# Seven block products in place of eight for the first matrix product of an MLP, inside a whole transformer layer

## The chip, the cores and the metric

The kernel runs on one core of one Trainium2 chip. The metric is the device time of one execution in microseconds (us), as the median of several runs. The core's engines are TensorE (PE), VectorE (DVE), ScalarE (ACT), GpSimd (POOL) and SyncE (SP, which here issues the DMA transfers). Each engine works off its own queue in order.

## What is computed

One layer over 2048 tokens of width 1024: a token mixer (RWKV and differential attention), then a gated MLP with a convolution over neighbouring tokens. The change touches the MLP alone:

```python
def conv_ffn(h, p):
    u = dwconv(h @ p['w_up'], p['ffn_conv']) + p['ffn_conv_b']     # w_up 1024 x 5632, three taps over tokens
    val, gate = jnp.split(u, 2, axis=-1)                           # 2816 columns each
    return (val * jax.nn.silu(gate)) @ p['w_down']                 # w_down 2816 x 1024

h = modulate(rmsnorm(x, p['g_pre_ffn']), sh2, sc2)
x = x + gt2 * rmsnorm(conv_ffn(h, p), p['g_post_ffn'])
```

All of it is in 32-bit floats.

## The kernel before

A matrix product of 32-bit numbers is made of three matmuls: each operand is split into a rounded part H and a rest L (`split`: ScalarE casts to H, then VectorE or GpSimd subtracts to get L), and `split_mm` adds H·H, H·L and L·H in PSUM. The kernel is written in a framework that puts in the waits between engines and chooses the order of the instructions in each engine's queue; the program gives an order of preference.

The function `phase45` is the MLP. Tokens go in 16 tiles of 128, or in 4 blocks of 512. Columns of w_up go in tiles of 128: column tile j (22 of them) has a half for `val` and one for `gate`.

First product. `ttiles` loads a tile of the residual stream x1, norms it (`row_stats`), transposes it on TensorE, scales it and splits it into the transposed activations, which all stay in SBUF (`h2H`, `h2L`, for the 4 blocks). The first four tiles are made while the phase before (`phase23`, the output projection of the mixer) is ending; the other twelve are made beside the matmuls of column tile 0. For each j and each half, `wload` loads 1024 x 128 weights (512 KB) and splits them, the subtraction on GpSimd; `mblock` runs 8 x 3 matmuls of 512 columns for each block and ScalarE copies the result to the tile `cs` (one row of 2048 tokens and a border on each side). `finish` makes the convolution and the gate from `cs` on VectorE (with one activation on ScalarE) in two pieces of 1024 tokens, and stores the result to DRAM (`actT`).

Second product. The 2816 rows of w_down are taken in two groups of 11 tiles. `dload` loads a row tile of w_down (512 KB) and splits it into the buffers that held h2H and h2L; `aload` loads and splits the activations of a token tile. For each group and token tile 11 x 2 x 3 matmuls run. The first group's results are copied to SBUF (`parts`); the second group's are added to them, normed and added to x1.

Of the kernel before, what the change touches and what calls it, by code (L numbers as in the profile page):

```python
# [8 lines left out]
F32 = mybir.dt.float32  # L9
# [1545 lines left out]
NH = NF // 2  # L1555
NT = SEQ // P
BORD = [0, 1, 2, 3]


def phase45(tc, I, T, pr, keep, ident, out):  # L1560
# [3 lines left out]
    st, sx = ExitStack(), ExitStack()  # L1564
    wp = st.enter_context(tc.tile_pool(name="wu", bufs=2, side="right"))
    hb = {BORD[0]: st.enter_context(tc.tile_pool(name="h2a", bufs=1, side="right"))}
    pss = [st.enter_context(tc.tile_pool(name="ps4a", bufs=1, space=PSUM, side="right"))]
    xp = sx.enter_context(tc.tile_pool(name="x4", bufs=1, side="right"))
    pt = sx.enter_context(tc.tile_pool(name="pst4", bufs=3, space=PSUM, side="right"))
    hH, hL = {}, {}  # L1570
# [3 lines left out]
    def pst():  # L1574
        pss.append(pss.pop(0))
        return pss[-1].tile([P, BLK], F32, name="o4")

    def new_h(b):
        hH[b], hL[b] = [hb[b].tile([P, KT, BLK], F32R, name="h2%s%d" % (s, b)) for s in "HL"]

    def wring():
        return (wp.tile([P, KT, P], F32, name="wuraw"), wp.tile([P, KT, P], F32R, name="wuH"), wp.tile([P, KT, P], F32R, name="wuL"))
# [5 lines left out]
    def wload(c0):  # L1588
        raw, H, L = wring()
        nc.sync.dma_start(out=raw, in_=wv[:, :, c0:c0 + P])  # L1590
        split(raw, H, L, nc.gpsimd)
        return H, L

    def stile(n):
        S = sp.tile([P, SEQ + 2], F32, name="cs%d" % n)
        nc.gpsimd.memset(S[:, 0:1], 0.0)
        nc.gpsimd.memset(S[:, SEQ + 1:SEQ + 2], 0.0)
        return S

    def mblock(W, S, b):  # L1600
        o = pst()
        for k in range(KT):
            split_mm(nc, o, W[0][:, k], W[1][:, k], hH[b][:, k], hL[b][:, k], k == 0, k == KT - 1)
            if k % 2 and k < KT - 1:
                yield
        nc.scalar.copy(out=S[:, 1 + b * BLK:1 + (b + 1) * BLK], in_=o)  # L1606
        yield

    def finish(j, Ss):
        for b in range(2):  # L1610
            t0 = b * 1024
            Os = []
            for n in (1, 0):
                w = [col[("fconvg%d" if n else "fconv%d") % t][:, j:j + 1] for t in range(3)]
                O = cv.tile([P, D], F32, name="co%d" % n)
                S = Ss[n]
                nc.vector.tensor_scalar(out=O, in0=S[:, t0:t0 + 1024], scalar1=w[0], scalar2=None, op0=ALU.mult)  # L1617
                nc.vector.scalar_tensor_tensor(out=O, in0=S[:, t0 + 1:t0 + 1025], scalar=w[1], in1=O, op0=ALU.mult, op1=ALU.add)
                nc.vector.scalar_tensor_tensor(out=O, in0=S[:, t0 + 2:t0 + 1026], scalar=w[2], in1=O, op0=ALU.mult, op1=ALU.add)
                if n:  # L1620
                    nc.scalar.activation(out=O, in_=O, func=AF.Silu, bias=col["fbias1"][:, j:j + 1])
                Os.append(O)
            nc.vector.scalar_tensor_tensor(out=Os[1], in0=Os[1], scalar=col["fbias0"][:, j:j + 1], in1=Os[0], op0=ALU.add, op1=ALU.mult)
            nc.sync.dma_start(out=T["actT"][j * P:(j + 1) * P, t0:t0 + 1024], in_=Os[1])

    tiles = [4 * b + t for b in BORD for t in range(4)]
    xq = {}

    def xload(m):
        if m < NT:  # L1630
            xq[m] = xp.tile([P, D], F32, name="xs4", bufs=4)
            nc.sync.dma_start(out=xq[m], in_=T["x1"][tiles[m] * P:(tiles[m] + 1) * P])

    def ttiles(m0, m1):
        for m in range(m0, m1):
            b, t = divmod(tiles[m], 4)
            z = (keep["gs2"], keep["sh2"], hH[b], hL[b], t * P, ident)
            transpose_half(nc, xp, pt, "tpx4", xq[m], 0, *z)
            if m + 2 < NT:
                row_stats(nc, xp, xp, xq[m + 2], mh)  # L1640
            yield
            transpose_half(nc, xp, pt, "tpx4", xq[m], 4, *z, nc.gpsimd)
            xload(m + 4)
            yield

    new_h(BORD[0])
    for m in range(4):
        xload(m)
    Ws = [wload(0), wload(DFF)]
    for m in range(2):  # L1650
        row_stats(nc, xp, xp, xq[m], mh)
    yield
    yield from ttiles(0, 4)
    yield "early"

    sp = st.enter_context(tc.tile_pool(name="cs4", bufs=1))
    hp = st.enter_context(tc.tile_pool(name="h2b", bufs=1))
    pss.extend([st.enter_context(tc.tile_pool(name="ps4b", bufs=4, space=PSUM))] * 4)
    for b in BORD[1:]:
        hb[b] = hp  # L1660
        new_h(b)
    Ss = [stile(0), stile(1)]

    def both(b):
        for n in range(2):
            yield from mblock(Ws[n], Ss[n], b)

    for m, b in enumerate(BORD):
        gens = [both(b)]
        if m < 3:  # L1670
            gens.append(ttiles(4 * m + 4, 4 * m + 8))
        robin(gens)
    sx.close()
    cv = st.enter_context(tc.tile_pool(name="cv", bufs=2))
    fp = st.enter_context(tc.tile_pool(name="fp5", bufs=1))
    pss.extend([st.enter_context(tc.tile_pool(name="ps4c", bufs=3, space=PSUM, side="right"))] * 3)
    finish(0, Ss)
    for j in range(1, NF):
        if j < NF - 1:
            Ss = []  # L1680
            for n in range(2):
                W = wload(n * DFF + j * P)
                S = stile(n)
                for b in range(4):
                    robin([mblock(W, S, b)])
                Ss.append(S)
        else:
            Ws = [wload(j * P), wload(DFF + j * P)]
            Ss = [stile(0), stile(1)]
            for n, b in ((0, 0), (0, 1), (1, 0), (1, 1), (0, 2), (0, 3), (1, 2), (1, 3)):  # L1690
                robin([mblock(Ws[n], Ss[n], b)])
        finish(j, Ss)

    acts, Wg = {}, {}

    def aload(a, t):
        r8, H8, L8 = wring()
        r3, H3, L3 = [fp.tile([P, NH - KT, P], d, name="a3" + s, bufs=2) for s, d in (("r", F32), ("H", F32R), ("L", F32R))]
        ts = slice(t * P, (t + 1) * P)
        nc.sync.dma_start(out=r8, in_=av[:, a * NH:a * NH + KT, ts])  # L1700
        nc.sync.dma_start(out=r3, in_=av[:, a * NH + KT:(a + 1) * NH, ts])
        split(r8, H8, L8, nc.gpsimd)
        split(r3, H3, L3, nc.gpsimd)
        acts[a, t] = [(H8[:, k], L8[:, k]) for k in range(KT)] + [(H3[:, k], L3[:, k]) for k in range(NH - KT)]

# [21 lines left out]
    for k in range(2, NH):  # L1727
        dload(0, k)
# [12 lines left out]
    for i, (a, t) in enumerate(steps):  # L1741
        if (a, t) == (0, NT - 3):
            draw(1, 0)
# [136 lines left out]
```

## Time and profile before

| | |
|---|---|
| time, median of 3 runs | 4140.62 us (4139.7 to 4144.2) |
| the profiled execution: span from first to last instruction | 4140.8 us |
| PE busy | 3824.6 us (92%), 25471 matmuls |
| DVE busy | 2671.8 us (65%) |
| ACT busy | 1881.5 us (45%) |
| POOL busy | 1543.3 us (37%) |
| moved by DMA | 400.80 MB, mean 97 GB/s |
| mean granted TensorE clock | 0.960 of full speed |

The profiled execution has nothing beside its span, which is as long as the median of the runs. A busy time is the sum of the durations of an engine's instructions, and a duration holds the time in which an instruction that has started stands still. Matmuls are pipelined: the records of neighbours overlap, so a matmul's cost is the distance to the next one, not its duration. "L1617" is a line of the kernel. `o<-h2H,wuH` names the tile that is written and those that are read.

### The profile page before, as it was taken

The page shows a single profiled execution, that of the slowest core. Times are in us where ns is not written, and L with a number is a line of the kernel's source. Part 1 is how long each engine was busy: PE and PEld are TensorE (multiplying, and loading weights), DVE is VectorE, ACT ScalarE, POOL GpSimd, SP SyncE. Part 2 cuts the span into 40 slices and gives each one's busy share as a digit, 9 for nine tenths or more (in the row PEclk, how much of TensorE's full clock was granted, in tenths as well). Part 3 has the DMA queues.
Part 4 walks back from the last instruction along what each step waited for, and adds up shares of the span by engine and source line. Part 5 has one row for each costly group of instructions (what it writes and reads, how often), then busy time and mean ns, then how long its engine had stood idle before and what let it go on. Part 6 is the DMA issues. An engine that isn't in the chain of part 4 may idle for free. (4 is left out here: it accounts for less than half of the span.)

```text
span 4140.8 us, 65493 instructions
## 1 busy us (share of the span) xinstructions
PE 3824.6 (92%) x25471; PEld 3213.6 (78%) x25471; DVE 2671.8 (65%) x3869; ACT 1881.5 (45%) x3678; POOL 1543.3 (37%) x1617
## 2 busy tenths in 40 slices
PE   7998888897899987989999899899999999999999
PEld 4777666676888876888898778788888888878887
DVE  3467678978889886888989868754444444420243
ACT  4235454466666656777777644521112112221211
POOL 3237467844444433455444366511101101022222
PEclk8999999998999988999999999999999999999999
DMA  4554546554434333020102163311111111131333
GB/s 174 160 168 154 162 146 214 205 161 94 97 95 101 94 85 101 8 61 22 33 6 74 51 219 136 117 61 51 46 43 62 46 41 56 51 101 44 115 114 102
DMA packets 464724, 400.80 MB, mean 97 GB/s; under 512 B 131613, under 2 KB 393702, under 8 KB 463390
## 3 DMA queue, kind: packets, MB, share of 16 engines
q1 hardware_dynamic: 464414, 396.61, 31.3%
q8 instruction: 201, 3.29, 0.3%
q14 instruction: 109, 0.89, 0.1%
HBM read 269.51 MB, written 131.74 MB: 97 GB/s over the span
## 5 line engine op out<-in xcount | busy, mean ns | idle before, releaser
L36 PE MATMUL o<-h2H,wuL 128*128 128x512 f32 x1920 | 761.7, 397 | 0.8 <-POOL wuL L1586 0.8
L34 PE MATMUL o<-h2H,wuH 128*128 128x512 f32 x1920 | 755.5, 394 | 5.6 <-DVE h2H L179 3.7
L35 PE MATMUL o<-h2L,wuH 128*128 128x512 f32 x1920 | 759.1, 395 | 0.2 <-DVE h2L L180 0.2
L1586 POOL TENSOR_TENSOR wuL<-wuraw,wuH 128x1024 fp32r<-128x1024 f32 x76 | 182.2, 2399 | 871.0 <-ACT wuH L1585 871.0
L34 PEld LDWEIGHTS o<-h2H,wuH 128*128 128x128 f32 x1920 | 362.0, 189 | 90.8 <-DVE h2H L179 3.9
L35 PEld LDWEIGHTS o<-h2L,wuH 128*128 128x128 f32 x1920 | 361.9, 189 | 89.9 <-DVE h2L L180 1.6
L36 PEld LDWEIGHTS o<-h2H,wuL 128*128 128x128 f32 x1920 | 362.1, 189 | 83.5 <-POOL wuL L1586 1.5
L34 PE MATMUL mm<-hH,wH 128*128 128x512 f32 (+1 forms) x968 | 384.5, 398 | 23.1 <-DVE hH L179 13.0
L787 DVE TENSOR_REDUCE nb<-S 128x1 f32<-128x768 f32 x384 | 357.8, 948 | 54.1 <-PE S L786 52.8
L35 PE MATMUL mm<-hL,wH 128*128 128x512 f32 (+1 forms) x968 | 382.0, 395 | 1.0 <-DVE rstd L162 0.9
L788 ACT ACTIVATE P<-S,nb 128x768 f32<-128x768 f32 x384 | 345.8, 907 | 77.4 <-DVE nb L787 74.5
L36 PE MATMUL mm<-hH,wL 128*128 128x512 f32 (+1 forms) x968 | 380.9, 394 | 0.0
L1617 DVE TENSOR_SCALAR co<-cs,cols 128x1024 f32<-128x1024 f32 x88 | 139.8, 1590 | 314.4 <-ACT cs L1606 313.0
L785 PE MATMUL S<-kH,qs 128*128 128x384 f32 x768 | 293.4, 382 | 36.1 <-ACT P L788 33.8
L829 PE MATMUL pv<-V,aT 128*128 128x128 f32 x2304 | 310.0, 279 | 5.5 <-DVE O L845 3.0
L1606 ACT COPY cs<-o 128x512 f32<-128x512 f32 x176 | 103.0, 586 | 449.8 <-PE o L36 449.6
L829 PEld LDWEIGHTS pv<-V,aT 128*128 128x128 f32 x2304 | 286.6, 195 | 9.1 <-DVE O L845 5.8
L786 PE MATMUL S<-kL,qs 128*128 128x384 f32 x768 | 261.2, 340 | 0.0
L815 DVE SCALAR_TENSOR_TENSOR P<-P,f,P 128x768 f32<-128x768 f32 x192 | 243.9, 1283 | 12.5 <-POOL P L813 10.9
L34 PEld LDWEIGHTS mm<-hH,wH 128*128 128x128 f32 x968 | 191.1, 198 | 63.8 <-DVE hH L179 13.9
L35 PEld LDWEIGHTS mm<-hL,wH 128*128 128x128 f32 x968 | 191.5, 198 | 40.2 <-DVE hL L180 2.2
L36 PEld LDWEIGHTS mm<-hH,wL 128*128 128x128 f32 x968 | 191.4, 198 | 38.9 <-issue 0.7
(362 smaller groups left out, 8103.6 us busy)
## 6 DMA issues: line engine op xcount, KB each, us to landing
wraw<-in_w_in_dram SPq DMA_DIRECT2D x52, 512.0 KB
wuraw<-in_w_up_dram SPq DMA_DIRECT2D x44, 512.0 KB
scr_actT<-co SPq DMA_DIRECT2D x44, 512.0 KB
QP<-scr_qd SPq DMA_DIRECT2D x36, 512.0 KB
PK<-scr_pd SPq DMA_DIRECT2D x144, 128.0 KB
mww<-in_w_mod_dram SPq DMA_DIRECT2D x64, 256.0 KB
scr_pd<-G SPq DMA_DIRECT2D x32, 512.0 KB
scr_qd<-Q SPq DMA_DIRECT2D x32, 512.0 KB
```

The source lines that it names most:

```text
L34: nc.tensor.matmul(out, lhsT=lH, rhs=rH, start=first, stop=False)
L35: nc.tensor.matmul(out, lhsT=lH, rhs=rL, start=False, stop=False)
L36: nc.tensor.matmul(out, lhsT=lL, rhs=rH, start=False, stop=last)
L785: nc.tensor.matmul(S[:, b, 0:HB], lhsT=qs[:, qt * P:(qt + 1) * P], rhs=kH[:, sl], start=True, stop=False)
L786: nc.tensor.matmul(S[:, b, 0:HB], lhsT=qs[:, qt * P:(qt + 1) * P], rhs=kL[:, sl], start=False, stop=True)
L787: nc.vector.tensor_reduce(out=nb[:, m, g:g + 1], in_=S[:, :, 0:HB], op=ALU.max, axis=AX.XY, negate=True)
L788: nc.scalar.activation(out=Pm[m][:, g * GW:(g + 1) * GW].rearrange("p (b x) -> p b x", b=2), in_=S[:, :, 0:HB], func=AF.Exp, bias=nb[:, m, ...
L815: nc.vector.scalar_tensor_tensor(out=Pm[0][:, sls[g - 1]], in0=Pm[0][:, sls[g - 1]], scalar=f[:, 0, g - 1:g], in1=Pm[1][:, sls[g - 1]], op ...
L829: nc.tensor.matmul(pv, lhsT=aT[:, j], rhs=V[:, k0 + j], start=(k0 + j == 0), stop=(k0 + j == KTT - 1))
L1586: eng.tensor_tensor(out=L, in0=raw, in1=H.bitcast(F32), op=ALU.subtract)
L1606: nc.scalar.copy(out=S[:, 1 + b * BLK:1 + (b + 1) * BLK], in_=o)
L1617: nc.vector.tensor_scalar(out=O, in0=S[:, t0:t0 + 1024], scalar1=w[0], scalar2=None, op0=ALU.mult)
```

## The change

The first product is made with the scheme of Strassen and Winograd, one level deep: the token blocks (rows of the result) are paired as block r = 0 and 1, the contraction of 1024 is halved (`HT` = 4 k tiles), and the two column halves are `val` and `gate`. Seven products of half-size operands replace eight. Their operands are sums and differences:

- activations (`convert`): seven combinations, made once for each token half s (1024 tokens) and kept in SBUF in H and L (`A[0]` to `A[6]`);
- weights (`wprep`): seven combinations for each column tile j, made anew for each token half, so that w_up is loaded twice. VectorE makes the four sums, ScalarE the casts, GpSimd the subtractions;
- results (`group`): the seven products (`prod`) go to three PSUM tiles a, b and c. Some are accumulated onto an earlier one, after this has been read: product 3 onto a (after ScalarE's copy p1), 4 and 6 onto b (after VectorE's sums u2 and u3), 5 onto c (after the copy p5). VectorE and GpSimd add up the four blocks of `cs`.

Loops: for s in 0, 1, for j in 0..21, one group of 7 products (7 x 4 x 3 matmuls of 512 columns). Column tile 0 of both token halves, and column tile 21 of the first, go in two groups of 256 columns. `finish` runs for each s and j over two pieces of some 512 tokens; a strip of two columns (`halo`) is kept for the second half. The normed, transposed activations go to DRAM (`hT`) and are loaded from there (`qload`). Eight token tiles are made beside the end of the phase before; the other eight beside the groups of column tiles 1 to 4 of the first half. Column tiles that are made ahead wait in a ring of 8 weight buffers.

The second product takes w_down in three groups of 8, 7 and 7 tiles (`KG`), so VectorE adds the second group's results too. Its raw rows have a ring of two buffers (`dr`).

```diff
+KG = [(0, 8), (8, 7), (15, 7)]
+HT = 4
...
+    def wprep(j, W):
+        B = {}
+        for r, c in ((0, 0), (0, 1), (1, 1), (1, 0)):
+            B[r, c] = wb()
+            c0 = c * DFF + j * P
+            nc.sync.dma_start(out=B[r, c], in_=wv[:, r * HT:(r + 1) * HT, c0:c0 + P])
+        yield
+
+        def put(raw):
+            H, L = wHL()
+            split(raw, H, L, nc.gpsimd)
+            W.append((H, L))
+        put(B[0, 0])
+        yield
+        T1 = wt()
+        sub(T1, B[0, 1], B[0, 0])
+        put(T1)
+        yield
...
+    def convert(rq, q, h):
+        cols = slice(h * 256, h * 256 + 256)
+
+        def put(i, raw):
+            split(raw, A[i][0][:, :, cols], A[i][1][:, :, cols], nc.gpsimd if i in (1, 4) else nc.vector)
+        put(0, q[0, 0])
+        yield
+        S1 = rq.tile([P, HT, 256], F32, name="sA")
+        nc.vector.tensor_tensor(out=S1, in0=q[1, 0], in1=q[1, 1], op=ALU.add)
+        put(1, S1)
+        yield
...
+    def finish(s, j, Ss, r):
...
+            O = sp.tile([P, BLK + 1], F32, name="co%d" % m, bufs=2 - m)[:, 0:n]
+            S = Ss[m]
+            nc.vector.tensor_scalar(out=O, in0=S[:, lo:lo + n], scalar1=w[0], scalar2=None, op0=ALU.mult)
+            for t in (1, 2):
+                nc.vector.scalar_tensor_tensor(out=O, in0=S[:, lo + t:lo + t + n], scalar=w[t], in1=O, op0=ALU.mult, op1=ALU.add)
...
+    def group(s, W, Ss, c0, n, steps):
+        a, b, c = [pst() for _ in range(3)]
...
+        def prod(i, o, first):
+            for x in steps:
+                next(x, None)
+            H, L = W[i]
+            for k in range(HT):
+                xH, xL = A[i][0][:, k, cols], A[i][1][:, k, cols]
+                for n3, (w, x) in enumerate(((H, xH), (H, xL), (L, xH))):
+                    nc.tensor.matmul(o[:, 0:n], lhsT=w[:, k], rhs=x, start=first and k + n3 == 0, stop=k == HT - 1 and n3 == 2,
+                                     skip_group_check=not first)
...
+        prod(0, a, True)
+        p1 = tmp("p1")
+        nc.scalar.copy(out=p1, in_=a[:, 0:n])
+        prod(1, c, True)
+        p5 = tmp("p5")
+        nc.scalar.copy(out=p5, in_=c[:, 0:n])
+        prod(2, b, True)
+        u2 = tmp("u2")
+        add(u2, b[:, 0:n], p1)
+        prod(3, a, False)
+        nc.scalar.copy(out=at(0, 0), in_=a[:, 0:n])
+        prod(4, b, False)
+        u3 = tmp("u3")
+        add(u3, b[:, 0:n], p1)
+        prod(5, c, False)
+        add(at(1, 0), c[:, 0:n], u2)
+        add(at(1, 1), u3, p5, nc.gpsimd)
+        prod(6, b, False)
+        add(at(0, 1), b[:, 0:n], p1)
...
     def draw(a, k):
-        if a and k % 3 == 0:
-            raw = fp.tile([P, D], F32, name="x5")
-        else:
-            raw = wp.tile([P, KT, P], F32, name="wuraw").rearrange("p a b -> p (a b)")
-        nc.sync.dma_start(out=raw, in_=dv[:, a * NH + k])
-        draws[a, k] = raw
+        draws[a, k] = fp.tile([P, D], F32, name="dr", bufs=2)
+        nc.sync.dma_start(out=draws[a, k], in_=dv[:, KG[a][0] + k])
...
-    steps = [(a, t) for a in range(2) for t in range(NT)]
+    steps = [(a, t) for a in range(3) for t in range(NT)]
```

## Rows read from the trace of the kernel before

**Rows 1.** The windows: busy time and instructions of each engine in three stretches.

```profile
core 0: us, PE busy (x) PEld busy (x) DVE busy (x) ACT busy (x) POOL busy (x), PEclk, DMA share, GB/s
2629.00:2705.00 76.00, 64.33 (x296) 50.35 (x295) 50.64 (x94) 46.14 (x106) 29.71 (x32) 0.91 0.30 97
2705.00:3641.00 936.00, 936.00 (x4032) 756.80 (x4031) 417.58 (x304) 192.33 (x261) 110.15 (x128) 1.00 0.15 51
3641.00:4133.00 492.00, 489.23 (x2110) 397.32 (x2108) 113.58 (x97) 96.87 (x141) 112.70 (x76) 0.99 0.30 95
```

**Rows 2.** By tile: count, ns shortest/median/longest, first and last start.

```profile
L34 PE MATMUL o<-h2H,wuH x1920: 387/392/794, 2629.2 to 4130.3; 128*128 128x512 f32 x192
...
L177 ACT ACTIVATE f<-tpx,sh,gs x96: 440/458/517, 2608.2 to 2690.6; 128x128 f32<-128x128 f32 x96
```

**Rows 3.** The timeline (start, us, engine, line): matmuls of 256 columns.

```profile
59.75 0.28 PE L35 MATMUL mm<-hL,wH 128*128 128x256 f32 x1
...
61.00 0.28 PE L34 MATMUL mm<-hH,wH 128*128 128x256 f32 x1
```

**Rows 4.** The timeline: a load's issue, and the cast that waits for it.

```profile
3878.47 0.35 SPq L1713 DMA_DIRECT2D x<-in_w_down_dram  x1
...
3882.15 1.05 ACT L1585 CAST h2H<-x 128x1024 fp32r<-128x1024 f32 x1 [2.23 <-DMA x<-in_w_down_dram]
```

**Rows 5.** By tile: durations of single operations of 512 and 1024 columns.

```profile
L179 DVE CAST h2H<-f x32: 412/424/2268, 2609.8 to 2691.1; 128x512 fp32r<-128x512 f32 x32
...
L180 DVE TENSOR_TENSOR h2L<-f,h2H x16: 676/691/2772, 2612.1 to 2690.0; 128x512 fp32r<-128x512 f32 x16
L180 POOL TENSOR_TENSOR h2L<-f,h2H x16: 1262/1290/1671, 2613.3 to 2691.6; 128x512 fp32r<-128x512 f32 x16
...
L1586 DVE TENSOR_TENSOR h2L<-wuraw,h2H x18: 1217/1225/1229, 3614.0 to 3899.2; 128x1024 fp32r<-128x1024 f32 x18
...
L1606 ACT COPY cs<-o x176: 566/588/615, 2642.5 to 3640.4; 128x512 f32<-128x512 f32 x176
L1617 DVE TENSOR_SCALAR co<-cs,cols x88: 746/755/2521, 2692.9 to 3641.5; 128x1024 f32<-128x1024 f32 x88
...
L1786 DVE SCALAR_TENSOR_TENSOR x<-cs,frs,x x5: 746/1284/3407, 4091.5 to 4137.0; 128x1024 f32<-128x1024 f32 x3, 128x512 f32<-128x512 f32 x2
```

**Rows 6.** The timeline of GpSimd and VectorE where a split meets `finish`.

```profile
2838.77 2.39 POOL L1586 TENSOR_TENSOR wuL<-wuraw,wuH 128x1024 fp32r<-128x1024 f32 x1 [16.39 <-ACT wuH L1585]
...
2839.22 2.50 DVE L1617 TENSOR_SCALAR co<-cs,cols 128x1024 f32<-128x1024 f32 x1 [2.57 <-ACT cs L1606]
```

**Rows 7.** The timeline of TensorE: transposes, and matmuls after a wait.

```profile
2643.31 1.03 PE L170 MATMUL tpx<-ident,xs 128*128 128x128 f32 x8
...
2689.53 1.22 PE L34 MATMUL o<-h2H,wuH 128*128 128x512 f32 x2 [3.66 <-DVE h2H L179]
...
2691.79 0.63 PE L34 MATMUL o<-h2H,wuH 128*128 128x512 f32 x1
```

**Rows 8.** The timeline of VectorE in an earlier stage, both queues full.

```profile
741.71 2.33 DVE L525 COPY wc<-t 128x8 f32<-128x8 f32 x1
743.96 1.81 DVE L551 SCALAR_TENSOR_TENSOR cout<-cst,cols,cout 128x512 f32<-128x512 f32 x1
745.69 1.75 DVE L527 SCALAR_TENSOR_TENSOR G<-t,kk 128x512 f32<-128x512 f32 x1
747.37 0.67 DVE L579 TENSOR_TENSOR kk<-kk,pk 128x512 f32<-128x512 f32 x1
```

**Rows 9.** The timeline of GpSimd in the same stretch.

```profile
741.20 2.81 POOL L233 TENSOR_TENSOR wL<-wraw,wH 128x1024 fp32r<-128x1024 f32 x1
743.97 1.25 POOL L533 TENSOR_TENSOR Q<-kk,t 128x504 f32<-128x504 f32 x1
745.18 1.71 POOL L535 TENSOR_TENSOR Q<-rr,t 128x512 f32<-128x512 f32 x1
746.87 1.05 POOL L519 TENSOR_SCALAR t<-t 128x512 f32<-128x512 f32 x1
```

More of the change, by code (lines that the diff above doesn't have):

```diff
@@ L1609, in finish @@
[L1609 to L1644, printed above, removed]
@@ L1678, in phase45, with sub @@
[L1678 to L1686, printed above, removed]
-        else:
[L1688 to L1692, printed above, removed]
+    def sub(o, x, y, eng=nc.vector):
+        eng.tensor_tensor(out=o, in0=x, in1=y, op=ALU.subtract)
@@ new lines, in stiles, with rqpool @@
+    def stiles(s, j):
+        Ss = [sp.tile([P, 1027], F32, name="cs%d" % m) for m in range(2)]
+        for m in range(2):
+            if s == 0:
+                nc.gpsimd.memset(Ss[m][:, 0:1], 0.0)
+            else:
+                nc.gpsimd.tensor_copy(out=Ss[m][:, 0:2], in_=halo[:, m, j])
+                nc.gpsimd.memset(Ss[m][:, 1026:1027], 0.0)
+        return Ss
+    def rqpool():
+        e = ExitStack()
+        return e, e.enter_context(tc.tile_pool(name="rawq", bufs=1, side="right"))
@@ new lines, in phase45 @@
+    tgen = iter(())
+    er, rq = rqpool()
+    q = qload(rq, 0, 0)
+    for s in range(2):
+        for j in range(NF):
+            Wn = []
+            wn = wprep((j + 1) % NF, Wn) if s == 0 or j < NF - 1 else iter(())
+            next(wn, None)
+            Ss = stiles(s, j)
+            if j == 0:
+                group(s, W, Ss, 0, 256, [convert(rq, q, 0)])
+                q = qload(rq, s, 1)
+                group(s, W, Ss, 256, 256, [convert(rq, q, 1), wn])
+                er.close()
+                if s == 0:
+                    ex = ExitStack()
+                    pt = ex.enter_context(tc.tile_pool(name="pst4b", bufs=2, space=PSUM, side="right"))
+                    x2 = ex.enter_context(tc.tile_pool(name="x4b", bufs=1, side="right"))
+                    tgen = ttiles(x2, 8, 16, 2)
+            elif s == 0 and j == NF - 1:
+                group(s, W, Ss, 0, 256, [])
+                group(s, W, Ss, 256, 256, [wn])
+            else:
+                group(s, W, Ss, 0, BLK, [wn, tgen])
+                if s == 0 and j == 4:
+                    for _ in tgen:
+                        pass
+                    ex.close()
+                    er, rq = rqpool()
+                    q = qload(rq, 1, 0)
+            for _ in wn:
+                pass
+            if s == 0:
+                for m in range(2):
+                    nc.gpsimd.tensor_copy(out=halo[:, m, j], in_=Ss[m][:, 1023:1025])
+            for r in range(2):
+                finish(s, j, Ss, r)
+            W = Wn
@@ L1694, in phase45 @@
+    fp = st.enter_context(tc.tile_pool(name="fp5", bufs=1, side="right"))
     acts, Wg = {}, {}
     def aload(a, t):
[L1697 to L1702, printed above, removed]
```

260 lines of the change are left out of this document (159 added, 101 removed).

## The prediction

> **What bounds the kernel now.** I read the windows first, cut at the stages of the MLP [rows 1]. From 2705 to 3641 us TensorE is busy for all 936 us at full granted clock, with 4032 matmuls, which is 21 column tiles of 192. One matmul of 512 columns therefore costs 936/4032 = 0.232 us and a column tile 44.6 us. VectorE is busy 45% there, ScalarE 21%, GpSimd 12%, the DMA engines 15%. The second product (3641 to 4133) is TensorE's too: 2110 of its 2112 matmuls are recorded, in 492 us. So in this part of the kernel a matmul taken away is worth its 0.232 us, as long as everything else stays below TensorE's pace. The one loose stretch is the first column tile, 2629 to 2705: TensorE has 64 us of busy time in 76, the clock is 0.91, because twelve of the sixteen token tiles are still being normed and transposed between its matmuls. It runs from the first matmul at 2629.2 [rows 2] to 2705, where the 21 x 192 begin: 76 us against 44.6.
>
> **The products taken away.** A column tile has 2 column halves x 4 token blocks x 8 k x 3 = 192 matmuls now, and 2 token halves x 7 products x 4 k x 3 = 168 after: 22 x 24 = 528 fewer, -122.5 us. I call 84 matmuls of one token half and one column tile a unit; there are 44, each 84 x 0.232 = 19.5 us. Three units go in halves of 256 columns. A 256-column matmul follows the last one by (61.00 - 59.75)/11 = 0.114 us, eleven matmuls on [rows 3], half of 0.232, so that costs nothing. The first tile's excess over 44.6 also goes, since transposes no longer stand between its matmuls: -31 us. Together -153.5.
>
> **The start.** Now the first matmul needs four token tiles in SBUF. After, it needs eight tiles, stored to DRAM, loaded again in another layout, combined and split. All sixteen tiles went from 2608.2 to 2690.6, 5.2 us each, beside matmuls [rows 2]; ScalarE's share of a new tile is four activations of 0.46, 1.8 us. With TensorE nearly free I take 4.1: eight tiles end at 2641. A 512 KB load took 3.7 us from its issue (3878.47) to the cast that waited for it (3882.15), and that cast 1.05 [rows 4]; one store and one load of half the size I take at 3.5 each. First matmul about 2649: +20 us (bounds 5, if tiles go at 2 us, and 30 at 5.2).
>
> The first unit is then paced by the conversion of the activations. One half (256 tokens of each block) has 4 combinations and 7 splits over 1024 elements: on VectorE 9 operations of 1.225, on GpSimd 2 of 2.39, on ScalarE 7 casts of 1.05 [rows 4 to 6]. For the reason below VectorE and GpSimd don't add up side by side, so a half takes 11.0 + 4.8 = 15.8, some 15. Two halves and the next tile's weight preparation (7 GpSimd splits of 1.29 and 4 subtractions of 0.69, 11.8) are 42 us where TensorE needs 19: +23 (bounds 0 and 25).
>
> **Eight more tiles** are normed beside the units 1 to 4: 64 transposes at about 0.11 (eight in 1.03 us) [rows 7] are 7 us on TensorE, and VectorE gets some 2.5 us for each tile, 20 in all. +10 (bounds 7 and 27).
>
> **The change of token half** converts 2 x 15.8 us again, between the last unit of the first half and the first of the second. Hidden it is 0, on full queues 30. VectorE's queue is nearly full, as the next part shows: +25.
>
> **The steady unit**, 41 of them, decides the sign. What VectorE has to do in one: the convolution and gate over two blocks, 10 scalar_tensor_tensor of 512 (0.75) and 4 tensor_scalar (0.42, from the cast of that size); 4 weight combinations (0.69); 4 adds with a PSUM operand (0.67) [rows 5, 8]. That is 7.5 + 1.7 + 2.8 + 2.7 = 14.7 us of 19.5. GpSimd has 7 splits of 512 at 1.29 and one add, 10.3 us. ScalarE has 7 casts of about 0.53, 3 evictions and 2 gates of under 0.6, below 7 us; it hides. Weights are read twice and the activations go through DRAM, some 40 MB more, under DMA engines that are busy 15%: costed at nothing while that share stays below a half. SP issues six transfers in a unit (four weight loads, two stores) at 0.35 us each [rows 4], 2.1 us of 19.5; a load held up behind a store that waits for `finish` has a unit of slack before its weights are used.
>
> But the two do not run beside each other. The GpSimd split from 2838.77 to 2841.16 met VectorE's tensor_scalar at 2839.22; that took 2.50 and ended 0.56 us after the split [rows 6], where alone it takes 0.75 [rows 5]. So VectorE stood until GpSimd was done and saved only about 0.2 of its own time. In a stretch where both queues are full the same is seen in turn [rows 8, 9]: from 741.71 to 747.44 VectorE's three operations take 2.33, 1.81 and 1.75 us beside three of GpSimd that wait as well (2.81 for one that takes 2.39 alone). Alone the six would be about 6.5 us (VectorE's first, 8 columns wide, is next to nothing), and they took 5.7: some 0.25 to 0.3 gained at each hand-over. The operation that reads PSUM at 747.37 runs its plain 0.67 beside the GpSimd operation that ends at 747.92, so such adds don't wait. Per unit: the 11.9 us of VectorE that wait for GpSimd, and 10.3, less 8 hand-overs at 0.3, are 19.8; half of the PSUM adds uncovered +1.4; operations that follow each other closely save some 0.08 each, -1.1; halo copies +0.2. That is 20.3 against TensorE's 19.5: +0.8 x 41 = +33 us. Bounds: 19.5 (all hidden), and 22.2 with nothing gained at a hand-over.
>
> The Trainium skill, SBUF — State Buffer, section "SBUF: two separate sides", goes further than these rows: it calls the pair of ports that VectorE and GpSimd share an exclusive lock, held for the whole instruction, the loser fully blocked. The collision above agrees as to who waits; the 0.2 to 0.3 us at each hand-over it does not grant. By that rule the unit would be 11.9 + 10.3 = 22.2 us and the sum 4181 us, by the rows 20.3 and 4103.
>
> Where this wait lands: within a group product 4 is accumulated onto the bank of product 2, and may start only when VectorE has added p1 to that bank (u2). In VectorE's queue stand, ahead of u2, the 14 operations of the unit before (finish) and two of its adds, which become ready when its product 5 ends. From there to the start of product 4 TensorE has 5 products, 14.0 us. The 17 operations alone are 11.3 us; two GpSimd splits among them fit, four or five don't. Products 4 to 6 and the next unit queue behind.
>
> **The second product** keeps its 2112 matmuls. There are two group changes in place of one, with two raw buffers of 512 KB where there were three; with 3.7 for the load, 1.05 and 1.23 for the splits a buffer turns round in 6.0 us, so the seventh row of a group comes some 2.5 to 3.5 us late: +7 for both. The first group no longer waits for the last activations: -2. The extra adds (32 at 0.67) run under matmuls. +5 (bounds 0 and 12).
>
> **The sum**, against the profiled execution's own 4140.8 us (the median of the runs is 4140.6): -122.5 - 31 + 20 + 23 + 10 + 25 + 33 + 5 = -37.5, so 4103 us.
>
> **Rivals.** First, VectorE and GpSimd fully in turn: the unit is 22.2 us, 41 x 2.7 = 111 in place of 33, and the time 4181, slower. It decides from a unit of 21.2 us, where 41 x 1.7 eats the 70 that the rest leaves. For it: every collision in the rows; the tensor_scalar that is blocked for the whole split; the position of u2. Against it: VectorE and GpSimd each have a unit of slack for the weights, and the hand-overs gain. Second, the pair fits: units at 19.5 to 19.8, 4070 to 4082. For it: GpSimd has only 8 operations, spread over the unit since each split waits for a weight buffer that a product frees; VectorE's own 14.7 us leave 4.8. Third, the fixed costs are twice what I take (start, conversions and switch 83 to 140 us) at a unit of 20.3: about no change. TensorE's waits can also cost clock: after a wait of 3.66 us its matmuls took 0.63 us in place of 0.39 [rows 2, 7], the lower of its two clock levels; at the start and the switch that adds some 2 us each, within the bounds.
>
> **How the numbers follow.** The forecast, a unit of 19.9 to 20.8 us, 4085 to 4130, has 0.42; the pair fits 0.22; fully in turn 0.28; the fixed costs doubled 0.08. Within 0.2% (8 us, about what a measurement of this kernel can tell from no change) lies the last alone. So faster 0.64, same 0.08, slower 0.28. The range goes from 4055 (the pair fits and the start costs 15 us less) to 4190 (in turn, a little over 22.2); I leave 0.07 below and 0.13 above.
>
> **What would show it.** Right: 7 products in one unit with matmuls 0.232 apart, the unit's period (two weight loads of equal rows apart) 19.9 to 20.8, TensorE's waits in the steady part mostly at product 4 on u2 and of about a microsecond; VectorE's tensor_scalar and scalar_tensor_tensor of 512 well over their 0.42 and 0.75 on the mean; the first matmul near 2649 and the first unit over 40 us. Wrong: a period of 19.5 (then the lock costs nothing and I am 33 us too high), a period above 21.2, waits at other products (on weights, or on ScalarE's p1), or a start or switch of 60 us.

## The result, and the profile after

The kernel after takes 4239.2 us (median of 4 runs, 4237.5 to 4240.5), the kernel before 4142.4 on the same chip (4 runs, 4139.7 to 4146.0): 1.0234 times as long, 95% interval 1.022 to 1.0249. Forecast were 4103 us, in a range of 4055 to 4190, with a chance of 0.64 for faster. The measured time lies above that range, and it is slower where faster was forecast.

Page of the kernel after, part 1: busy time, share of the span and instructions of each engine, over a span of 4235.6 us.

```profile
PE 3780.5 (89%) x25195; PEld 3161.4 (75%) x25195; DVE 3159.4 (75%) x4593; ACT 2011.0 (47%) x3979; POOL 2003.0 (47%) x2040
```

The windows, which answer to [rows 1]: two steady stretches (13 units of the first token half, some 11 of the second), and the second product.

```profile
core 0: us, PE busy (x) PEld busy (x) DVE busy (x) ACT busy (x) POOL busy (x), PEclk, DMA share, GB/s
2893.00:3195.00 302.00, 271.30 (x1124) 215.37 (x1123) 261.92 (x289) 90.48 (x160) 163.70 (x156) 0.94 0.23 69
3300.00:3560.00 260.00, 232.67 (x937) 182.71 (x936) 222.14 (x248) 74.49 (x134) 138.33 (x135) 0.95 0.23 70
3728.00:4228.00 500.00, 497.09 (x2127) 398.39 (x2127) 125.00 (x149) 108.04 (x179) 126.36 (x111) 1.00 0.30 93
```

TensorE, which was busy for all of 936 us before, is busy 90% of the first steady stretch, and VectorE 87%: no engine is full. DMA stands at 0.23. A unit's period is read from two ScalarE copies of product 0 (p1), in the timeline of ScalarE:

```profile
3009.38 0.59 ACT L1757 COPY p<-o 128x512 f32<-128x512 f32 x1
...
3032.55 0.59 ACT L1757 COPY p<-o 128x512 f32<-128x512 f32 x1
```

So the unit is 23.2 us (23.1 in the second half), where the forecast had 20.3. Who waits for whom in the 13 units from 2893 to 3195 (us in all, times, longest), TensorE and VectorE:

```profile
PE o L1746 <- DVE u L1753: 28.3, 13, 3.4
...
DVE co L1722 <- ACT cs L1765: 22.1, 12, 1.8
DVE co L1722 <- POOL cs L1753: 14.1, 12, 1.2
```

TensorE waits for VectorE, as foreseen, but VectorE itself stands idle once in a unit for ScalarE and once for GpSimd. These two rows are what the prediction did not have, and they are all of VectorE's list in that stretch: it has no wait for TensorE. The timeline of VectorE over most of one unit (start, duration; in brackets the idle time before, and what ended it):

```profile
3001.02 0.67 DVE L1753 TENSOR_TENSOR u<-o,p 128x512 f32<-128x512 f32 x1
3001.62 0.73 DVE L1728 SCALAR_TENSOR_TENSOR co<-co,cols,co 128x511 f32<-128x511 f32 x1
3003.54 1.50 DVE L1722 TENSOR_SCALAR co<-cs,cols 128x512 f32<-128x512 f32 x1 [1.19 <-POOL cs L1753]
3005.08 1.80 DVE L1724 SCALAR_TENSOR_TENSOR co<-cs,cols,co 128x512 f32<-128x512 f32 x1
...
3020.24 1.14 DVE L1722 TENSOR_SCALAR co<-cs,cols 128x511 f32<-128x511 f32 x1 [1.84 <-ACT cs L1765]
3021.41 1.64 DVE L1724 SCALAR_TENSOR_TENSOR co<-cs,cols,co 128x511 f32<-128x511 f32 x1
...
3024.24 0.68 DVE L1753 TENSOR_TENSOR u<-o,p 128x512 f32<-128x512 f32 x1
```

The first wait is for the sum u3 + p5 (the block `at(1, 1)`), on GpSimd, and it can only start when VectorE has made u3:

```profile
3001.78 1.73 POOL L1753 TENSOR_TENSOR cs<-u,p 128x512 f32<-128x512 f32 x1 [2.49 <-DVE u L1753]
```

The second is for `at(0, 0)`, ScalarE's copy of product 3's bank into the first block of `val`. In ScalarE's queue it stands behind the gate's silu and a weight cast, and the silu (the activation of the gate) waits 7.49 us for VectorE's last tap of the gate (a tap is one of the convolution's three products):

```profile
3018.49 0.72 ACT L1726 ACTIVATE co<-co,cols 128x511 f32<-128x511 f32 x1 [7.49 <-DVE co L1724]
3019.12 0.60 ACT L1583 CAST wH<-wt 128x512 fp32r<-128x512 f32 x1
3019.63 0.58 ACT L1765 COPY cs<-o 128x512 f32<-128x512 f32 x1
```

TensorE then waits at product 6, for u3, and loses its clock for a while. In its timeline a matmul follows the last at 0.23 before the wait and at 0.42 to 0.43 behind it, at the lower of the two clock levels (the granted clock is 1.00 from 3010 to 3021 and 0.50 from 3025 to 3030):

```profile
3020.98 0.40 PE L1746 MATMUL o<-aH,wH 128*128 128x512 f32 x1
3021.21 0.39 PE L1746 MATMUL o<-aL,wH 128*128 128x512 f32 x1
3024.97 0.79 PE L1746 MATMUL o<-aH,wH 128*128 128x512 f32 x1 [3.37 <-DVE u L1753]
...
3025.99 0.63 PE L1746 MATMUL o<-aH,wL 128*128 128x512 f32 x1
3026.41 0.63 PE L1746 MATMUL o<-aH,wH 128*128 128x512 f32 x1
```

Last, the stretch from 2893 to 3195 by shape (count; busy, mean ns; idle before): VectorE's operations and GpSimd's splits beside each other. Alone a scalar_tensor_tensor takes 750 and GpSimd's split 1290 ns [rows 5]. For the tensor_scalar the forecast took the 420 of a cast; run 8 below, with the splits off GpSimd, has it at 480.

```profile
L1724 DVE SCALAR_TENSOR_TENSOR co<-cs,cols,co 128x512 f32<-128x512 f32 x53 | 65.5, 1235 | 1.0
...
L1722 DVE TENSOR_SCALAR co<-cs,cols 128x511 f32<-128x511 f32 x26 | 30.6, 1177 | 23.4 <-ACT cs L1765 22.1
...
L1753 DVE TENSOR_TENSOR u<-o,p 128x512 f32<-128x512 f32 x26 | 17.6, 678 | 0.0
...
L1584 POOL TENSOR_TENSOR wL<-wt,wH 128x512 fp32r<-128x512 f32 x51 | 66.0, 1294 | 50.6 <-ACT wH L1583 50.4
L1584 POOL TENSOR_TENSOR wL<-wb,wH 128x512 fp32r<-128x512 f32 x39 | 60.3, 1546 | 16.7 <-ACT wH L1583 16.6
```

VectorE is busy 261.92/13 = 20.15 us in a unit and waits (22.1 + 14.1)/13 = 2.8; with small gaps that is 23.2. Its own work is 14.7 by the forecast's prices, so some 5.5 of the 20.15 are spent standing still inside operations that GpSimd holds up. The sums that read PSUM (where the matmuls leave their results) keep their plain 0.68.

**The theory** for the runs: VectorE's queue sets the unit, at 14.7 of its own work, 5.5 of standing still and 2.8 to 3.0 of waits. **Rivals**: TensorE's wait for u3, with the slow matmuls behind it, is part of the loop that sets the period; the standing still beside GpSimd does not matter and the queue of ScalarE sets it; the doubled weight loads pace the units.

### The profile page after: what moved, and what is told of

Read it like the earlier page. It is cut to its first block, busy times and chain, and to the rows that moved or that the text cites. A ratio compares the mean times of both kernels' runs of the same rounds, so it can differ in the third digit from the quotient of the medians.

```text
span 4235.6 us, 67772 instructions
## 1 busy us (share of the span) xinstructions
PE 3780.5 (89%) x25195; PEld 3161.4 (75%) x25195; DVE 3159.4 (75%) x4593; ACT 2011.0 (47%) x3979; POOL 2003.0 (47%) x2040
## 5 line engine op out<-in xcount | busy, mean ns | idle before, releaser
L1746 PE MATMUL o<-aH,wH 128*128 128x512 f32 (+1 forms) x1316 | 519.0, 403 | 128.1 <-DVE u L1753 96.3
L1746 PE MATMUL o<-aL,wH 128*128 128x512 f32 (+1 forms) x1316 | 522.0, 397 | 2.6 <-POOL aL L1584 1.3
L1746 PE MATMUL o<-aH,wL 128*128 128x512 f32 (+1 forms) x1316 | 516.0, 398 | 0.0
L1584 POOL TENSOR_TENSOR wL<-wb,wH 128x512 fp32r<-128x512 f32 x228 | 324.4, 1424 | 376.7 <-ACT wH L1583 370.9
L1746 PEld LDWEIGHTS o<-aH,wH 128*128 128x128 f32 x1316 | 263.0, 200 | 207.9 <-DVE u L1753 116.0
L1724 DVE SCALAR_TENSOR_TENSOR co<-cs,cols,co 128x512 f32<-128x512 f32 (+2 forms) x352 | 377.4, 1074 | 5.8
L1746 PEld LDWEIGHTS o<-aH,wL 128*128 128x128 f32 x1316 | 263.3, 200 | 56.3
L35 PE MATMUL o<-aL,wH 128*128 128x512 f32 x704 | 277.4, 395 | 0.7 <-DVE aL L1584 0.7
L36 PE MATMUL o<-aH,wL 128*128 128x512 f32 x704 | 277.4, 395 | 0.0
L34 PE MATMUL o<-aH,wH 128*128 128x512 f32 x704 | 275.3, 395 | 0.0
```

What stands on the lines that cost most here:

```text
L34: nc.tensor.matmul(out, lhsT=lH, rhs=rH, start=first, stop=False)
L35: nc.tensor.matmul(out, lhsT=lH, rhs=rL, start=False, stop=False)
L36: nc.tensor.matmul(out, lhsT=lL, rhs=rH, start=False, stop=last)
L1584: eng.tensor_tensor(out=L, in0=raw, in1=H.bitcast(F32), op=ALU.subtract)
L1724: nc.vector.scalar_tensor_tensor(out=O, in0=S[:, lo + t:lo + t + n], scalar=w[t], in1=O, op0=ALU.mult, op1=ALU.add)
L1746: nc.tensor.matmul(o[:, 0:n], lhsT=w[:, k], rhs=x, start=first and k + n3 == 0, stop=k == HT - 1 and n3 == 2, skip_group_check=not first)
```

## The experiments

Each is the kernel after with the edit shown. The unit is the distance of two p1 copies in the steady part of the first half (where they alternate, the mean), the time the median, the ratio that to the kernel before on the same chip.

| | edit | time, us | ratio, 95% interval | unit, us |
|---|---|---|---|---|
| | the kernel after | 4239.2 | 1.0234 (1.022 to 1.0249) | 23.2 |
| 1 | two matmuls in place of three | 4121.0 | 0.9939 (0.9924 to 0.9954) | some 20.1 |
| 2 | L of the weights by a ScalarE cast | 4073.3 | 0.9827 (0.9812 to 0.9841) | 19.60 |
| 3 | first tap on ScalarE | 4160.4 | 1.0033 (1.002 to 1.0047) | 21.07 |
| 4 | sum u3 + p5 on VectorE | 4216.8 | 1.0172 (1.0157 to 1.0187) | 22.6 |
| 5 | copy of product 3 on VectorE | 4225.9 | 1.0199 (1.0181 to 1.0216) | 22.8 |
| 6 | 4 and 5 | 4198.0 | 1.0138 (1.012 to 1.0156) | 22.03 |
| 7 | 4, 5, and four `wt` buffers | 4162.3 | 1.005 (1.0033 to 1.0067) | 21.02 |
| 8 | weight splits on VectorE | 4090.4 | 0.9871 (0.9857 to 0.9886) | 19.60 |
| 9 | 3 and 8 | 4078.0 | 0.9843 (0.9825 to 0.9861) | 19.60 |
| 10 | four `f` buffers at the start | 4232.3 | 1.0214 (1.0199 to 1.0229) | 23.2 |
| 11 | 3, 8 and 10 | 4068.7 | 0.9825 (0.9809 to 0.984) | 19.60 |
| 12 | 11, conversions on VectorE | 4065.9 | 0.982 (0.9802 to 0.9838) | 19.60 |

**1. A third less work for TensorE.** The flag that ends a product's sum moves with it.

```diff
-for n3, (w, x) in enumerate(((H, xH), (H, xL), (L, xH))):
+for n3, (w, x) in enumerate(((H, xH), (L, xH))):
```

> The kernel after, with one of the three matmuls of every k step of the seven products left out (H of the weights by L of the activations), so the first product is not the full one: 56 matmuls in a unit, 13.0 us of TensorE in place of 19.5; VectorE, GpSimd and ScalarE keep every operation. The unit after is 23.2 us. Theory (VectorE's queue sets the unit: 14.7 us of its own, 5.5 of standing still beside GpSimd, 3.0 of waits for ScalarE's copy and GpSimd's sum): the unit stays 22.8 to 23.3, the time 4220 to 4240, and only TensorE's waits grow. Rival (TensorE's wait for u3 and the lower clock after it are part of the loop that sets the period): the unit falls by 3 us or more, the time to 4120 or below. Rival (the DMA of weights read twice paces the units): no change either, but then VectorE's waits are for loads.

The unit fell to some 20.1 us and the time to 4121, so the theory as it stood there, that it stays, fell too. It is nearly what the rival of TensorE's loop had forecast: a fall of 3 us or more, and 4120 or below. The window of this kernel:

```profile
2900.00:3100.00 200.00, 155.92 (x555) 117.04 (x554) 197.92 (x219) 71.58 (x121) 133.74 (x120) 0.87 0.25 78
```

And VectorE's longest waits from 2893 to 3195:

```profile
DVE wt L1587 <- POOL wL L1584: 1.6, 1, 1.6
DVE co L1722 <- DMA scr_actT<-co: 1.5, 3, 0.9
DVE u L1753 <- ACT p L1757: 0.9, 2, 0.6
```

VectorE is now 99% busy. At 22 operations a unit the 219 in 200 us are 9.95 units of 20.1 us: its busy time of before the edit, without the waits. (From one p1 copy to the next the units alternate here, and the means of longer stretches lie between 19.8 and 20.7.) With shorter products the framework ordered VectorE's queue in another way: it has other operations to make while ScalarE's copy of product 3 and GpSimd's sum are made, and neither is among its waits. So this run shows VectorE's floor beside GpSimd, and the theory needed a second half: the 3 us of waits are no fixed part of VectorE's work. What brings them, TensorE's pace or the order, this run can't tell; runs 4 to 7 speak to it.

**2. GpSimd's weight splits out of the way.** L then holds a copy of the weight.

```diff
-            split(raw, H, L, nc.gpsimd)
+            nc.scalar.copy(out=H, in_=raw)
+            nc.scalar.copy(out=L, in_=raw)
```

> The kernel after, with the rest L of the weights written by a second ScalarE cast in place of GpSimd's subtraction (so L holds another value: a copy of the weight), which takes seven of GpSimd's eight operations out of a unit and adds 7 x 0.58 = 4.1 us to ScalarE. Theory (VectorE stands still beside GpSimd): VectorE's operations fall to their own 14.7 us plus at most 1 us beside the one GpSimd sum left, the 3.0 us of waits for ScalarE and GpSimd stay or grow a little, so the unit is TensorE's, 19.5 to 20.0, and the time 4085 to 4110. Rival (the waits for ScalarE's copy set the unit, the port does not): 23 us or more, since ScalarE has more to do ahead of that copy; 4235 to 4280.

The unit is TensorE's 19.60 and the time 4073, some 12 us under the range. In the window TensorE is busy all the time at full clock and VectorE 153 of 200 us, 15.0 a unit; by its waits (second fence) it waits more than ever for ScalarE's copy, up to 3.2 us, which costs nothing while the unit has room:

```profile
2900.00:3100.00 200.00, 200.00 (x875) 161.41 (x875) 153.05 (x226) 112.80 (x196) 26.87 (x51) 1.00 0.26 80
```

```profile
DVE co L1723 <- ACT cs L1766: 30.9, 11, 3.2
DVE cs L1754 <- PE o L1747: 19.3, 14, 1.6
```

The rival that puts everything on ScalarE's queue is out, and so is that of the loads, which are as many at a faster pace.

**3. The first tap on ScalarE.**

```diff
-nc.vector.tensor_scalar(out=O, in0=S[:, lo:lo + n], scalar1=w[0], scalar2=None, op0=ALU.mult)
+nc.scalar.activation(out=O, in_=S[:, lo:lo + n], func=AF.Identity, scale=w[0])
```

> The kernel after, with the first tap of the convolution (four tensor_scalar in a unit, 0.42 us each alone, 0.96 to 1.18 on the mean in the steady part) made by ScalarE as an activation with a scale. Nothing is left out. Theory (they cost VectorE their time with the port waits, 4.3 us in a unit): VectorE is busy 16 us, the unit 19.6 to 20.6, the time 4100 to 4135. Rival (VectorE and GpSimd take their turns, so only the 4 x 0.42 = 1.7 us of VectorE's own go and the port waits fall on the operations behind): the unit 21.3 to 21.8, the time 4160 to 4185. Rival (VectorE then waits for ScalarE's taps in place of making them): 22.5 or more, 4210 to 4260.

The unit fits none of the three: 21.07 us (21.24 in the second half). The time of 4160.4 lies at the lower edge of the second one's 4160 to 4185. VectorE is busy 159.97 of 200 us, 16.85 a unit, which is 3.3 less than 20.15 where 4.3 were expected and 1.7 by the rival; and the waits for ScalarE's copy and GpSimd's sum gave way to waits for ScalarE's taps, 39.0 us in the 9.5 units from 2900 to 3100, 4.1 a unit. 16.85 + 4.1 = 21.0.

```profile
2900.00:3100.00 200.00, 191.57 (x802) 148.69 (x801) 159.97 (x173) 88.65 (x153) 124.90 (x114) 1.00 0.24 74
```

```profile
DVE co L1724 <- ACT co L1722: 39.0, 28, 2.0
```

**4. The sum u3 + p5 on VectorE.**

```diff
-add(at(1, 1), u3, p5, nc.gpsimd)
+add(at(1, 1), u3, p5)
```

> The kernel after, with the fourth sum of a unit (u3 + p5) made by VectorE in place of GpSimd (1.73 us there, 0.68 here). Nothing is left out. Theory (VectorE waits 1.17 us a unit for this sum): 0.7 us more of its own, 1.2 less of waiting and some 0.3 less beside GpSimd, so the unit is 22.2 to 22.7 and the time 4200 to 4220. Rival (that wait is slack, and VectorE's busy time counts): 23.5 to 23.9, 4250 to 4270. Rival (TensorE's own loop): no change.

As the theory had it: 22.6 us and 4217. The wait for GpSimd is gone, the one for ScalarE's copy stays and is VectorE's only wait from 2893 to 3195. The window and that wait:

```profile
2900.00:3100.00 200.00, 179.61 (x731) 141.34 (x730) 182.34 (x206) 58.68 (x103) 100.55 (x98) 0.96 0.23 70
```

```profile
DVE co L1722 <- ACT cs L1765: 22.5, 12, 1.9
```

**5. The copy of product 3 on VectorE.**

```diff
-nc.scalar.copy(out=at(0, 0), in_=a[:, 0:n])
+nc.vector.tensor_copy(out=at(0, 0), in_=a[:, 0:n])
```

> The kernel after, with the copy of product 3's bank into the first block of val made by VectorE in place of ScalarE. Nothing is left out. In the kernel after it stands in ScalarE's queue behind the gate's silu and a cast, and VectorE waits 1.84 us a unit for it. Theory (the order of ScalarE's queue costs this wait; the bank itself is ready some 3 us earlier): VectorE gets 0.68 us more to do and loses 1.84 of waiting, the unit falls from 23.2 to 21.8 to 22.4, the time from 4239 to 4180 to 4210. Rival (product 3 itself is late, TensorE sets the period): VectorE waits for TensorE in its place, the unit stays 23 or more, 4230 to 4270.

22.8 us and 4226, between the theory's ranges and the rival's. The wait for the copy went, VectorE did not wait for TensorE instead (so product 3 was not late), but a wait of 1.2 us came up that the expectation did not have, for a GpSimd split that holds one of the three buffers of combined weights:

```profile
DVE wt L1587 <- POOL wL L1584: 14.2, 12, 1.2
DVE co L1722 <- POOL cs L1753: 14.2, 12, 1.2
```

It has the same root: that split waits for a weight cast that stands in ScalarE's queue behind the silu.

**6 and 7. Both on VectorE, then a fourth buffer for the combined weights** (with one raw buffer less, to make room).

```diff
-        return wp.tile([P, HT, P], F32, name="wb", bufs=5)
+        return wp.tile([P, HT, P], F32, name="wb", bufs=4)
...
-        return wp.tile([P, HT, P], F32, name="wt", bufs=3)
+        return wp.tile([P, HT, P], F32, name="wt", bufs=4)
```

> The kernel after, with both on VectorE: the copy of product 3's bank and the sum u3 + p5. Nothing is left out; GpSimd keeps the seven weight splits. VectorE has 14.7 + 2 x 0.68 = 16.1 us of its own. Theory (the unit is VectorE's busy time beside GpSimd and what is left of its waits): seven splits cost it some 4.8 us of standing still, the two waits of 1.84 and 1.17 are gone, of the wait of 1.2 for a weight buffer that came up with the copy alone nothing or all is left: 20.9 to 22.1 us, 4150 to 4195. Rival (TensorE's own loop over u3 holds the unit up): 22.5 or more, 4210 to 4230.

> The kernel after, with the copy of product 3's bank and the sum u3 + p5 on VectorE, and with four buffers in place of three for the combined weights (the raw weights get four in place of five, to make the room). Nothing is left out. With the copy and the sum alone the unit was 22.0 us, of which VectorE waited 1.18 for a split of GpSimd that held the third buffer. Theory (the unit is VectorE's busy time beside GpSimd plus whatever it waits): the wait goes, the unit is 20.8 to 21.2, the time 4150 to 4170. Rival (the wait turns up elsewhere, since ScalarE's casts behind the silu release the splits): still 21.8 to 22.2, 4190 to 4205. Rival (loads now come late with four raw buffers): VectorE or ScalarE waits for loads, 22.5 or more.

Run 6 gave 22.03, in the range for the unit (with all of the 1.2 us left), and 4198, 3 us above the range for the time. Run 7 gave 21.02 and 4162, both in the range: the wait for the buffer went, and nothing but 0.7 us for a load took its place. In runs 4, 6 and 7 TensorE has the same 84 matmuls in a unit; with edits to the other engines' work and buffers alone the unit fell from 23.2 to 22.6, 22.03 and 21.02. By the windows (23 operations a unit in run 4, 24 in runs 6 and 7) VectorE was busy 20.4, 20.5 and 19.9 us of these, so that what fell is its idle time: from 3.05 us a unit to 2.2, 1.5 and 1.1. With no wait of VectorE for TensorE in the kernel after and the unit moving with VectorE's idle time, TensorE's loop is out. One view of the kernel after seems to speak for it: the chain of work that the profile follows back goes through 50 matmuls from 3024.97 to 3039.58. But it comes to them from a GpSimd split that began at 3042.98, 3.4 us behind them and right behind ScalarE's cast of 3042.30, so that link is slack. The windows of runs 6 and 7, and VectorE's longest wait from 2893 to 3195 in each:

```profile
2900.00:3100.00 200.00, 184.93 (x756) 145.65 (x756) 186.26 (x218) 57.48 (x99) 103.66 (x100) 0.97 0.24 73
2900.00:3100.00 200.00, 189.65 (x798) 149.71 (x797) 189.99 (x229) 59.25 (x105) 116.25 (x105) 0.99 0.24 74
```

```profile
DVE wt L1587 <- POOL wL L1584: 14.2, 12, 1.2
DVE wt L1587 <- DMA wb<-in_w_up_dram: 6.6, 10, 0.7
```

**8. The weight splits on VectorE.**

```diff
-            split(raw, H, L, nc.gpsimd)
+            split(raw, H, L, nc.vector)
```

> The kernel after, with the seven weight splits of a unit on VectorE in place of GpSimd. Nothing is left out. VectorE then has 14.7 + 7 x 0.69 = 19.5 us of its own, against 20.2 busy beside GpSimd. Theory (GpSimd's splits cost VectorE 5.5 us of standing still): VectorE's operations take their plain times, the unit is 19.5 plus what is left of the 3.0 us of waits: 20.5 to 22.8, the time 4130 to 4220. Rival (VectorE's long operations are its own): 23.2 + 4.8 = 28 us, over 4400.

One word changes the sign: 19.60 us and 4090, better than the 20.5 to 22.8 expected, 1.3% below the kernel before. The window, and VectorE's scalar_tensor_tensor of 512 columns in it:

```profile
2900.00:3100.00 200.00, 200.00 (x859) 160.64 (x858) 193.11 (x300) 74.06 (x124) 28.94 (x51) 1.00 0.28 83
```

```profile
L1724 DVE SCALAR_TENSOR_TENSOR co<-cs,cols,co 128x512 f32<-128x512 f32 x40 | 29.7, 744 | 0.2
```

VectorE makes seven more operations in a unit and is busy 193.11/200 x 19.6 = 18.9 us, less than the 20.15 with GpSimd's help; the operation that took 1235 ns takes 744. Beside run 2, which has neither GpSimd's splits nor VectorE's, this prices the seven: 20.15 - 15.0 = 5.1 us of VectorE's busy time where GpSimd makes them, 18.9 - 15.0 = 3.9 where VectorE does. The waits for the copy and the sum are gone: here too the framework put the queues in another order. Part of the gain is therefore the order's; the floor of VectorE alone went from 20.1 (run 1) to 18.9.

**9. Both, splits on VectorE and first taps on ScalarE.**

> Both: the weight splits on VectorE, and the four first taps of a unit on ScalarE. Nothing is left out. VectorE has 14.7 - 1.7 + 4.8 = 17.8 us of its own and stands beside GpSimd for one sum alone. Theory (VectorE's queue sets the unit, and ScalarE's taps cost VectorE waits of up to 4 us a unit as they do beside GpSimd): the unit is 19.6 (TensorE) to 21.5, the time 4075 to 4150. Rival (the waits for ScalarE's taps come on top in full): 22 us, 4170 to 4190.

The unit stays at TensorE's 19.60, and the time is 4078, both in the theory's ranges; the rival's 22 us is out. That is 12 us less than run 8. Of these, 7.7 come in the five units beside which the eight token tiles are made, where VectorE has their work as well: from 2719.62 to 2832.82 in run 8, 113.2 us, and from 2718.69 to 2824.23 in run 9, 105.5.

**10. Four buffers for the half tiles on their way to DRAM.**

```diff
-f = xp.tile([P, 4, P], F32, name="f", bufs=2)
+f = xp.tile([P, 4, P], F32, name="f", bufs=4 if bufs == 4 else 2)
```

> The kernel after, with four buffers in place of two for the normed, transposed half tiles on their way to DRAM, for the first eight token tiles. Nothing is left out. VectorE waits 8 us in all there for a store to leave its buffer. Theory (the stores pace the start): the first matmul of the MLP comes at about 2656 in place of 2664, the time is 4228 to 4235. Rival (the loads of the tiles or the phase before pace it): no change, 4237 to 4241.

4232, in the theory's range, but the interval of the ratio overlaps that of the kernel after, so a gain is not shown; and the theory's reason is not what happened. VectorE's 8.4 us of waits for these stores are gone, and yet the first matmul of the MLP came at 2662.8, 0.7 earlier and not 8. Between the two profiled executions lie 3.6 us (4232.0 and 4235.6), of which 3.1 are there at the last p1 copy (3725.75 and 3728.89), gathered little by little; where the rest of the 7 between the medians comes from, if it is one, is open.

**11 and 12. The best of these together, then the conversions' two GpSimd splits of a half on VectorE too.**

```diff
-split(raw, A[i][0][:, :, cols], A[i][1][:, :, cols], nc.gpsimd if i in (1, 4) else nc.vector)
+split(raw, A[i][0][:, :, cols], A[i][1][:, :, cols], nc.vector)
```

> The weight splits on VectorE, the first taps on ScalarE, and four buffers for the half tiles at the start. Nothing is left out. Theory (units at TensorE's pace, so what is left is the start): 7 us less than with the first two alone (4078), 4068 to 4073. Rival (the first unit's conversions take the start's gain back): 4076 to 4080.

> The same, and the conversion of the activations with all seven splits of a half on VectorE in place of two on GpSimd. Nothing is left out. Theory (GpSimd's two splits of 2.39 us hold VectorE up for longer than the 2 x 1.225 it would take itself): 2.3 us less for each of four halves, 4058 to 4066. Rival (the first unit waits for loads and casts, and VectorE's 2.4 us more come on top): 4070 to 4082.

4068.7 as expected, 9 us under run 9, though the intervals overlap. Here the ring does what run 10 was to show: the first matmul of the MLP comes at 2652.2, where run 9 has 2662.3, and VectorE has no wait for these stores before it. Then 4065.9, inside the theory's 4058 to 4066, but the intervals do not tell it from 4068.7. From the first matmul to the p1 copy of unit 20 run 12 is 4.4 us shorter (3085.44 - 2652.19 in run 11, 3088.10 - 2659.24 in run 12; 2.7 of it up to the first p1 copy of full width), and at the change (to the second unit of the second half) 3.9, 79.4 and 75.5. Together that is near the 9.2 expected of the conversions; but the first matmul came 7 us later, with nothing changed ahead of it but the order. The best version is 1.8% faster than the kernel before. Its units are TensorE's, so what the change costs now is the start and the change of token half.

## Why the prediction was wrong

By its terms, against the profiled execution's 4235.6 us (132.6 above the forecast):

| step | forecast, us | measured, us |
|---|---|---|
| the start (first matmul of the MLP) | 2649 | 2663.6, +14.6 |
| the first unit | 42 | some 42, 0 |
| eight more tiles | +10 | +11 |
| the change of token half | +25 | +23 |
| the steady unit | 20.3 | 23.2, +126 over 43 units (41 x 2.9, and 2 that were taken at 19.5) |
| the second product | +5 | -1.5, -6.5 |

Measured by p1 copies are the tiles, five units from 2719.45 to 2846.50 less 5 x 23.2, and the change, three units from 3171.93 to 3264.37, 92.4 less 3 x 23.2. The first unit is the next one's p1 copy at 2719.45 less the 60 matmuls of 0.232 us that TensorE had then made of later units, from 2663.6. The second product is 498.3 us against 499.8 before, counted from where 36 more matmuls, those left of the first product behind the last p1 copy (3728.89), would end at 0.232 us each. The steps add up to 133.

**The step that failed is the steady unit.** Its prices held, but VectorE's waits, 2.8 to 3.0 us a unit, were left out. "That is 20.3 against TensorE's 19.5" summed VectorE's own work and its standing still beside GpSimd; that sum is confirmed twice, by the 20.15 us busy in the kernel after and by the 20.1 of run 1, where VectorE had nothing else. What failed is the sentence on ScalarE: "below 7 us; it hides". Its 7 us do hide, but one operation of them, the copy of product 3, stands in a queue behind a silu that waits for VectorE's own last tap, and then VectorE waits for it: a loop through two queues. The same holds for GpSimd's sum, which I counted for its duration and not for its place, between u3 and the operation that needs it. An operation off the busiest engine's list still costs its latency when that engine is both its cause and its customer. Runs 4 to 7 priced both, and the wait for a buffer hidden behind them: taking all three away is worth 2.2 us a unit and 77 us in all. An order of ScalarE's queue with the copy ahead of the silu was not run.

**The first rival** had the sign, but its price (4181, at 22.2 us) is 58 us short of the measured time, and its mechanism is not what happened. By the Trainium skill's SBUF — State Buffer, section "SBUF: two separate sides", the shared pair is held for the whole instruction, and the unit would be 11.9 + 10.3 = 22.2 us of VectorE and GpSimd in turn. Run 1 shows VectorE, GpSimd's eight operations beside it, done in 20.1. So who waits is as the Trainium skill has it, and an estimated (22.2 - 20.1)/8 = 0.26 us are gained at each hand-over. That the forecast's 0.25 to 0.3 fits is in part luck: from the start of the first GpSimd operation (741.20) to 747.44 the six operations of [rows 8, 9] took 6.2 us and not 5.7, which leaves at most 0.1 for a hand-over; only the 0.2 of [rows 6] stands.

**The third rival** was priced wrong in the forecast: with 140 us of fixed costs in place of 83 its sum is 4160, 0.5% slower and not about no change. By the table they came to some 89 (34 + 23 + 11 + 23 - 2).

**What GpSimd's help costs** was right in the sum and went unused. Eight GpSimd operations cost VectorE some 5.5 us of standing still in a unit, 0.7 each; VectorE makes such a subtraction itself in 0.68 when nothing holds it up. So GpSimd's help was worth nothing, and with its 1.3 us of latency it added waits. The prediction priced it at 5.6 us (20.3 - 14.7) and did not ask what the same work costs where it is not moved. The Trainium skill says in Perfetto Trace Analysis, section "Optimizing Scalar/DVE Operations", that moving work from VectorE to GpSimd may not help because they share a read port; run 8 agrees: without it the kernel is 149 us faster, part of that by the order of the queues.

**Where the wait lands.** Foreseen at product 4 on u2; it is at product 6 on u3. The prediction followed the order of the program text; the framework mixes the products of neighbouring units (from 2695.28 in the trace, matmuls of 512 columns, of the next unit, stand between the 256-column ones of the first). That u2 had time by this is not shown by a run. The clock falls behind these waits (0.94 granted on the mean of the steady part), as the third rival's last sentence had it, but in the steady part no cost of it shows: VectorE sets the unit and has no wait for TensorE, TensorE waits 28.3/13 = 2.2 us a unit, and in runs 2 and 8 the clock is back at 1.00.

**What was right.** The products taken away, the first unit, the tiles, the change of half, loads that hide (DMA 0.23). The start was 15 us worse. The load is as foreseen, 3.8 us from its issue (2658.70) to the cast (2662.46); it is the eight tiles that end late, some 15 us after the 2641 that 4.1 us a tile gave. VectorE's `f` waits there for the stores of a ring of two, 0.7 to 2.0 us each, but in run 10 the ring alone did not cure it, in run 11 it went with a start 10 us earlier, and run 12 shows that the order alone moves this start by 7 us.

## What to carry to other kernels

When work is added to an engine near its limit, sum its own operations, its standing still beside a helper engine, and then every wait in which it is both the cause and the customer of another queue's operation; the last term is not in any busy time, and here it was 2.8 of 23.2 us. Before giving a helper engine work that holds up the busy one, set the helper's price to it (0.7 us an operation here) beside the time it takes itself (0.68 here). A scheme with fewer matmuls pays only while everything around it stays under TensorE's new, shorter pace: the same seven products are 2.3% slower than the kernel before or, with three kinds of helper operations on other engines and one ring of buffers longer (run 12), 1.8% faster.

## What the runs showed of the hardware

VectorE's sums with an operand in PSUM keep 0.68 us beside a running GpSimd operation (run 1 too: 680 to 681 ns on the mean), while a scalar_tensor_tensor out of SBUF goes from 0.74 to 1.24 on the mean (0.97 for the one of 511 columns). A copy out of PSUM that was moved onto a nearly full VectorE (runs 5 to 7) cost its plain 0.685. The sum of two SBUF tiles cost 0.68 in the steady part as well, where it stood in the queue; that it would elsewhere is not shown. After a wait of 3.4 us TensorE ran some 13 matmuls at 0.42 to 0.43 us apart before it came back to 0.23, and the granted clock was 0.94 on the mean of such units; in run 7, with waits of at most 2.3 us and 10.4 in 200 us, it was 0.99.
